# One transpose of the input instead of two: the residual rebuilt from the normalised rows

## The chip, the core and the metric

The kernel runs on one NeuronCore of a Trainium2 chip. The metric is the device time of one launch in microseconds (us), as the median of three runs. The core has five engines that run side by side, each through its own list of instructions in order: PE multiplies matrices and transposes, ACT and DVE read what PE leaves in its accumulator banks (PSUM), POOL works on the on-chip memory (SBUF) alone, and SP issues DMAs. "PEld" in the profile is PE's load of the stationary operand.

## What is computed

One layer of a decoder, for 1024 prompt rows and 32 sample rows (8 sequences of 4 tokens), D = 1024:

```python
def mixer_inputs(x, pos, ln_w, w_in, ...):
    z = rmsnorm(x, ln_w) @ w_in            # rmsnorm: x * rsqrt(mean(x*x) + EPS) * w
    ...                                    # retention q/k/v/gate, MLA latents, gates
def finish_layer(x, ret_o, rg, mla_o, mg, ga, gb, ple, ...):
    h_ret = retention_out(ret_o, rg, ret_gn_w) @ w_down_ret
    h_mla = (mla_o * jax.nn.silu(mg)) @ w_down_mla
    merged = jax.nn.sigmoid(ga) * h_ret + jax.nn.sigmoid(gb) * h_mla
    x = x + merged @ w_out                 # the residual: raw x
    return x + jax.nn.sigmoid(x @ w_ple_gate) * (ple @ w_ple_proj)
```

So the raw rows x are needed twice: normalised at the start, and unchanged as the residual of the output projection near the end.

## The kernel before, in words

All 1056 rows (NT) are kept transposed: features on the 128 partitions, rows along the free axis. Every product is computed in three passes with operands split into a high and a low part (`mac`, L262 to L268: high by high, high by low, low by high).

**The head (L332 to L469).** The rows come in nine tiles of 128 (the ninth, tile 8, has the 32 sample rows). `norm_tile(t)` (L332) squares and sums a tile on ACT (L337), gets the reciprocal root r of each row through `rstd_of` (L233, L235, on POOL but for the first tile), and then makes two transposed copies:

- the raw one: `turn_input` (L314) transposes the eight 128x128 blocks of the tile on PE (L322) in two halves of four, each half into one PSUM bank of the kind `tr` (there are three), ACT copies each bank to SBUF (L323), and SP stores it to the scratch tensor xTD in DRAM (L324);
- the normalised one: DVE multiplies the rows by r (L340, tile xs), PE transposes the eight blocks (L345), again in two banks, and for each block ACT writes the high part times the weight of the norm (L350, xh) and DVE the low part (L351, xl). These stay in SBUF as the operand xn of all input projections.

`latent_tile(t)` (L373) then multiplies the tile by the latent weights, 24 matmuls of 384 columns and 24 of 320 into two banks `ac` (also three). ACT, POOL and DVE normalise and rotate the result (L385, L233, L235, L387, L361 to L366), PE transposes it five times (L396, L398, two banks `tr`), ACT and DVE copy it out (L400, L401). `turn_p(t)` (L326) transposes the tile of a second input with two more transposes through the same `turn_input` (tile names pl and pTD). The tiles go in the order 0, 1, 8, 2, 3, 4, 5, 6, 7, and `norm_tile` runs two tiles ahead of `latent_tile`. From the seventh tile on, the gate projections (`fill`, L421) are woven in.

**The end (L1303 to L1377).** The down projections are merged, and the output projection runs for eight feature blocks f: while block f multiplies, SP loads block f+1 of xTD (`x_transposed`, L1298, from a pool `w4` with three slots), and DVE adds it to each third of the product (L1365). Tiles of the size of one block come from a pool of 23 slots (`xs_`).

**What sets the order.** The program text gives priorities. A list scheduler walks it ahead of the run with estimated times, gives out slots and banks as they come free in that estimate, and writes one fixed list of instructions for each engine; at run time an engine goes through its list in order and waits where an instruction is not ready. So a change of the text can change the order on every engine.

Of the kernel before, what the change touches and what calls it, by code (L numbers as in the profile page):

```python
# [9 lines left out]
F32 = mybir.dt.float32  # L10
# [4 lines left out]
ALU = mybir.AluOpType  # L15
# [4 lines left out]
P = 128  # L20
D = 1024
# [4 lines left out]
NT = SEQ + NR  # L26
# [128 lines left out]
def run(g):  # L155
    for _ in g:
        pass
# [3 lines left out]
def decode_step(ctx: ExitStack, tc: tile.TileContext, A: dict, O: dict):  # L161
    nc = tc.nc
    pe, act, dve, pool, sp = nc.tensor, nc.scalar, nc.vector, nc.gpsimd, nc.sync
# [3 lines left out]
    dram = ctx.enter_context(tc.tile_pool(name="scratch", bufs=1, space=DRAM))  # L167
# [11 lines left out]
    def tr():  # L179
        return banks["pool"].tile([P, 512], F32, tag="tr", name="tr", bufs=3)  # L180
# [6 lines left out]
    def slots(pl, tag, bufs):  # L187

        return lambda name, shape=(P, NT), dt=F32R: pl.tile(list(shape), dt, tag=tag, name=name, bufs=bufs)

    def b32(ap):
        return ap.bitcast(F32)
# [26 lines left out]
    vD = [dram.tile([P, NT], F32, tag=f"v{f}", name=f"v{f}") for f in range(4)]  # L219
    latD = dram.tile([P, 5, SEQ], F32, tag="latD", name="latD")  # L220
    xTD = dram.tile([P, 8, NT], F32, tag="xTD", name="xTD")
    pTD = dram.tile([P, 2, NT], F32, tag="pTD", name="pTD")
    krD = dram.tile([P, 8, ROPE], F32, tag="krD", name="krD")

# [2 lines left out]
    def small(pl, tag, w=1, bufs=4):  # L227
        return pl.tile([P, w], F32, tag=tag, name=tag, bufs=bufs)

    def rstd_of(pl, ss, n, scale, by=pool, w=1):  # L230

        v = small(pl, f"rs_v{w}", w, 4 if w == 1 else 2)
        by.tensor_scalar(v[:n], ss[:n], scale, EPS, op0=ALU.mult, op1=ALU.add)  # L233
        r = small(pl, f"rs_r{w}", w, 4 if w == 1 else 2)
        pool.tensor_tensor(out=r[:n], in0=v[:n], in1=nhalf[:n].to_broadcast([n, w]), op=ALU.pow)  # L235
        return r
# [16 lines left out]
    def load_w(src, nk):  # L253

        hi, lo = wtiles()
        src = src.rearrange("(k p) f -> p k f", p=P)
        for k in range(0, nk, 4):
            ks = slice(k, min(k + 4, nk))
            stage(src[:, ks], hi[:, ks], lo[:, ks])
        return hi, lo  # L260
# [9 lines left out]
    def gemm(w, xs, evac, nk, thirds_=range(3)):  # L270

        for j in thirds_:
            ps = mm()
            sl = slice(j * TH, (j + 1) * TH)
            for k in range(nk):
                mac(ps[:, :TH], (w[0][:, k, :], w[1][:, k, :]), (xs[k][0][:, sl], xs[k][1][:, sl]), k == 0, k == nk - 1)
                if k == nk - 1:
                    evac(j, ps[:, :TH], sl)
                yield 0.441
# [6 lines left out]
    p1 = ph.enter_context(tc.tile_pool(name="p1", bufs=2))  # L286
# [3 lines left out]
    def rows(t):  # L290
        return P if t < 8 else NR
# [22 lines left out]
    def turn_input(t, src, dst, nf):  # L314

        n = rows(t)
        for half in range(0, nf, 4):
            st = p1.tile([P, 4, P], F32, tag="turn", name="turn", bufs=4)
            w = min(4, nf - half)
            pt = tr()  # L320
            for i in range(w):
                pe.transpose(pt[:, i * P:i * P + n], src[:n, (half + i) * P:(half + i + 1) * P], ident[:n, :n])  # L322
            act.copy(st[:, :w, :n], pt[:, :w * P].rearrange("p (a b) -> p a b", a=w)[:, :, :n])  # L323
            sp.dma_start(dst[:, half:half + w, t * P:t * P + n], st[:, :w, :n])  # L324
# [7 lines left out]
    def norm_tile(t):  # L332
        n = rows(t)
        xt = xts.pop(t)
        ss = small(p1, "ss")
        xs = p1.tile([P, D], F32, tag="xs", name="xs", bufs=2)
        act.activation(xs[:n], xt[:n], AF.Square, accum_out=ss[:n])  # L337
        r = rstd_of(p1, ss, n, 1.0 / D, dve if t == 0 else pool)
        turn_input(t, xt, xTD, D // P)
        dve.tensor_scalar(xs[:n], xt[:n], r[:n], None, op0=ALU.mult)  # L340
        for half in range(2):
            pt = tr()
            for q in range(4):
                k = half * 4 + q
                pe.transpose(pt[:, q * P:q * P + n], xs[:n, k * P:(k + 1) * P], ident[:n, :n])  # L345
            for q in range(4):
                k = half * 4 + q
                src = pt[:, q * P:q * P + n]
                hi = xn[k][0][:, t * P:t * P + n]
                act.activation(hi, src, AF.Copy, scale=lnw[:, k:k + 1])  # L350
                dve.scalar_tensor_tensor(out=xn[k][1][:, t * P:t * P + n], in0=src, scalar=lnw[:, k:k + 1],  # L351
                                         in1=b32(hi), op0=ALU.mult, op1=ALU.subtract)

    def rope_nat(out, z, t, n, pl, nh, tag):

        cos = ropeM[:n, t, 0:32].unsqueeze(1).to_broadcast([n, nh, 32])
        sin = ropeM[:n, t, 32:64].unsqueeze(1).to_broadcast([n, nh, 32])
        t1 = pl.tile([P, nh, 32], F32, tag=tag + "1", name=tag + "1", bufs=1)
        t2 = pl.tile([P, nh, 32], F32, tag=tag + "2", name=tag + "2", bufs=1)
        x1, x2 = z[:, :, 0:32], z[:, :, 32:64]  # L360
        dve.tensor_tensor(out=t1[:n], in0=x1, in1=cos, op=ALU.mult)  # L361
        dve.tensor_tensor(out=t2[:n], in0=x2, in1=sin, op=ALU.mult)
        dve.tensor_tensor(out=out[:, :, 0:32], in0=t1[:n], in1=t2[:n], op=ALU.subtract)
        dve.tensor_tensor(out=t1[:n], in0=x2, in1=cos, op=ALU.mult)
        dve.tensor_tensor(out=t2[:n], in0=x1, in1=sin, op=ALU.mult)
        dve.tensor_tensor(out=out[:, :, 32:64], in0=t1[:n], in1=t2[:n], op=ALU.add)  # L366
# [68 lines left out]
    sp.dma_start(cst[:, :head], A["consts"][:, :head])  # L435
    sp.dma_start(lnw, A["ln_w"][0].rearrange("(f p) -> p f", p=P))
    norm_tile(0)
    order = [0, 1, 8, 2, 3, 4, 5, 6, 7]
    for k in range(8):
# [4 lines left out]
    sp.dma_start(kvw, A["kv_norm_w"][0:1, :].to_broadcast([P, KL]))  # L444
    sp.dma_start(ropeM, A["ropeM"])
    norm_tile(order[1])
    load_x(order[3])

    def latents():
        due = iter(())  # L450
        for n, t in enumerate(order):
            tile_ = latent_tile(t)
            next(tile_, None)
            run(due)
            due = tile_
            if n + 2 < 9:
                norm_tile(order[n + 2])
            if n + 4 < 9:
                load_x(order[n + 4])
            turn_p(t)  # L460
            if n == 1:
                sp.dma_start(cst[:, head:], A["consts"][:, head:])
                sp.dma_start(gnw, A["ret_gn_w"][0].rearrange("(f p) -> p f", p=P))
            if n == 4:
                page_rows()
            yield 7.1 if n > 5 else 0.0
        run(due)
# [523 lines left out]
    def split(raw, hi, lo):  # L991
        act.copy(hi, raw)
        lo_of(lo, raw, hi)
        return hi, lo
# [236 lines left out]
    for h in range(HM):  # L1231
# [15 lines left out]
        for n, m in enumerate((3, 2, 0, 1)):  # L1247
            back = waiting.pop(0) if waiting and (h + 1 < HM or n != 1) else iter(())
# [24 lines left out]
    xs_, w4 = slots(pz, "x", 23), slots(pz, "w4", 3)  # L1273
# [14 lines left out]
    def load_gated(f, pl):  # L1288
        lo = gated(f, pl)
        return split_gated(pl("gh"), lo)  # L1290

    def gate(src, f):
        t = w4("gate", dt=F32)
        sp.dma_start(t, src[f])
        act.activation(t, t, AF.Sigmoid)
        return t

    def x_transposed(f):  # L1298
        xT = w4("xT", dt=F32)
        sp.dma_start(xT, xTD[:, f, :])  # L1300
        return xT

    M, gx = [], []  # L1303
    for f in range(8):
# [3 lines left out]
        out = M[f]  # L1308
# [9 lines left out]
    for half in range(2):  # L1318
        for f in range(8):
            w = load_w(A["w_down_ret"][0, half * 1024:(half + 1) * 1024, f * P:(f + 1) * P], 8)  # L1320
            ga = gate(gaD, f)
            if half:
                merged.append((xs_("mh"), xs_("ml")))

            def evac(j, ps, sl, f=f, ga=ga, half=half):
                t = wst.tile([P, TH], F32, tag="gev", name="mev", bufs=2)
                dve.tensor_tensor(out=t, in0=ps, in1=ga[:, sl], op=ALU.mult)
                out = M[f][:, sl]
                dve.tensor_tensor(out=out, in0=out, in1=t, op=ALU.add)
                if half:  # L1330
                    split(out, merged[f][0][:, sl], merged[f][1][:, sl])
            if half and f == 7:
                nxt_xT = x_transposed(0)
            run(gemm(w, gx, evac, 8))
            if half == 0:
                nxt.append(load_gated(8 + f, xr_))
        gx = nxt
# [18 lines left out]
    for f in range(8):  # L1356
        fs = slice(f * P, (f + 1) * P)
        xT = nxt_xT
# [125 lines left out]
```

## Time and profile before

| | us |
|---|---|
| median of 3 runs | 2250.8 |
| lowest, highest run | 2250.61, 2253.29 |
| the profiled execution | 2248.48 |
| its span, first to last instruction | 2246.7 |
| PE busy in the span | 2192.1 |

The trace gives start and length of each instruction in us from the start of the span. A row of the timeline reads: start, length, engine, line, operation, tile written and tiles read, form, count, and in brackets the idle time of the engine before it with what ended it. Matmuls are pipelined: the length of one (0.3 us) is longer than the step from one to the next, so costs on PE are taken from starts.

### The profile page before, as it was taken

What the parts mean: (1) busy time and instruction counts of PE and PEld (TensorE: products, weight loads), DVE (VectorE), ACT (ScalarE), POOL (GpSimd) and SP (SyncE); (2) the same over time, 40 slices, a digit from 0 to 9 for tenths busy, and PEclk for the clock granted to TensorE, in tenths of its full rate; (3) what the DMA queues carried; (4) which work ended last, traced back from release to release, by engine and by line L of the source; (5) the groups of instructions that cost most, each with busy time, mean ns of one, the idle gap of its engine ahead of it and who ended that gap; (6) DMA issues with size and microseconds to landing.
All of it is one profiled execution on the core that took longest, in us unless ns stands there. A gap on an engine that the chain in (4) does not pass through costs nothing.

```text
span 2246.7 us, 45040 instructions
## 1 busy us (share of the span) xinstructions
PE 2192.1 (98%) x18482; PEld 1975.0 (88%) x18482; DVE 1207.9 (54%) x2624; ACT 709.8 (32%) x1532; POOL 509.9 (23%) x682
## 2 busy tenths in 40 slices
PE   8899999999999999999999999999999999999997
PEld 7898888888888899798798779888887999999997
DVE  5414454444544438728638447767767344454465
ACT  6312112222322123222222122355456332222243
POOL 2224434344444114203203102122222000000021
PEclk9999999999999999999999999999999999999999
DMA  8446565656565442532613753200110453333243
GB/s 234 131 148 247 184 223 174 227 183 222 182 232 178 153 135 59 165 99 66 212 49 95 237 162 87 81 23 24 37 46 27 149 192 106 96 94 107 87 141 114
DMA packets 293391, 303.65 MB, mean 135 GB/s; under 512 B 29760, under 2 KB 242048, under 8 KB 293184
## 3 DMA queue, kind: packets, MB, share of 16 engines
q1 hardware_dynamic: 268608, 216.86, 31.3%
q0 software_dynamic: 24576, 83.90, 10.8%
q8 instruction: 145, 2.38, 0.4%
q14 instruction: 62, 0.51, 0.1%
HBM read 234.76 MB, written 65.94 MB: 134 GB/s over the span
## 4 chain that ended last, share of the span: by engine, by line
PE 82%; DVE 7%; issue 6%; POOL 3%; ACT 2%; DMA 1%; SPq 0%; POOLq 0%; ACTq 0%; DVEq 0%
PE mm L266 19%; PE mm L268 18%; PE mm L267 18%; PE sc L640 5%; PE x L667 3%; PE mm L1199 2%; PE ac L267 2%; PE ac L268 2%; PE ac L266 2%; PE tr L1186 1%; PE ac L936 1%; PE ac L932 1%; DVE Stl L198 1%; PE ac L1139 1%; PE tr L791 1%
## 5 line engine op out<-in xcount | busy, mean ns | idle before, releaser
L266 PE MATMUL mm<-xh,wh 128*128 128x352 f32 x1728 | 577.4, 334 | 0.2 <-ACT qq L523 0.2
L268 PE MATMUL mm<-xh,wl 128*128 128x352 f32 x1728 | 562.4, 325 | 0.0
L267 PE MATMUL mm<-xl,wh 128*128 128x352 f32 x1728 | 560.5, 324 | 0.0
L266 PEld LDWEIGHTS mm<-xh,wh 128*128 128x128 f32 x1728 | 324.6, 188 | 38.4 <-issue 29.5
L268 PEld LDWEIGHTS mm<-xh,wl 128*128 128x128 f32 x1728 | 325.5, 188 | 18.6 <-issue 17.3
L267 PEld LDWEIGHTS mm<-xl,wh 128*128 128x128 f32 x1728 | 325.8, 189 | 14.5 <-issue 7.2
L198 DVE TENSOR_TENSOR wl<-wr,wh 128x512 fp32r<-128x512 f32 (+2 forms) x283 | 189.0, 679 | 202.4 <-ACT wh L247 175.7
L247 ACT CAST wh<-wr 128x512 fp32r<-128x512 f32 x248 | 149.8, 619 | 356.0 <-PE mm L267 319.2
L634 DVE STREAM_TRANSPOSE kt<-craw 128x512 f32<-128x512 f32 x256 | 159.3, 679 | 151.0 <-PE sc L640 150.4
L413 ACT ACTIVATE gev<-mm 128x352 f32<-128x352 f32 x132 | 61.1, 463 | 357.2 <-PE mm L268 256.7
L584 POOL DMA_INDIRECT rraw<-in_cache_krope_dram,idx x128 | 123.7, 966 | 215.4 <-DVE kt L634 166.2
L585 POOL DMA_INDIRECT craw<-in_cache_ckv_dram,idx x128 | 120.5, 941 | 142.6 <-PE x L667 102.2
L640 PE MATMUL sc<-kt,q 32*32 32x256 f32 x5120 | 125.5, 385 | 0.1
L266 PE MATMUL mm<-mh,wh 128*128 128x352 f32 x384 | 124.3, 324 | 0.8 <-DVE M L1309 0.8
L267 PE MATMUL mm<-ml,wh 128*128 128x352 f32 x384 | 124.5, 324 | 0.0
L268 PE MATMUL mm<-gh,wl 128*128 128x352 f32 x384 | 124.3, 324 | 0.0
L266 PE MATMUL mm<-gh,wh 128*128 128x352 f32 x384 | 124.3, 324 | 0.0
L268 PE MATMUL mm<-mh,wl 128*128 128x352 f32 x384 | 124.2, 324 | 0.0
L267 PE MATMUL mm<-gl,wh 128*128 128x352 f32 x384 | 124.1, 323 | 0.0
L1415 POOL TENSOR_TENSOR xr<-x1h,x1l 128x352 f32<-128x352 f32 x24 | 26.1, 1106 | 404.7 <-PE mm L268 367.0
L640 PEld LDWEIGHTS sc<-kt,q 32*32 32x32 f32 x5120 | 75.1, 103 | 34.0 <-issue 9.5
L1164 POOL TENSOR_SCALAR pr<-pr,rl 128x896 f32<-128x896 f32 (+3 forms) x64 | 49.7, 777 | 133.3 <-DVE rl L1163 91.0
(351 smaller groups left out, 4294.4 us busy)
## 6 DMA issues: line engine op xcount, KB each, us to landing
wr<-in_w_in_dram SPq DMA_DIRECT2D x144, 256.0 KB, 3.6
st<-in_state_ret_dram SPq DMA_DIRECT2D x32, 512.0 KB, 5.2
out_ret_sample_dram<-st SPq DMA_DIRECT2D x32, 512.0 KB, 3.3
wr<-in_w_ple_gate_dram SPq DMA_DIRECT2D x48, 256.0 KB, 3.0
gt<-gev SPq DMA_DIRECT2D x48, 176.0 KB, 3.3
gl<-go SPq DMA_DIRECT2D x16, 528.0 KB, 4.2
gate<-ga SPq DMA_DIRECT2D x16, 528.0 KB, 3.5
g<-gt SPq DMA_DIRECT2D x32, 256.0 KB, 3.2
```

The lines of the kernel that those rows point to most:

```text
L198: dve.tensor_tensor(out=out, in0=src, in1=b32(hi), op=ALU.subtract)
L247: hi_by[0](hi, raw)
L266: pe.matmul(out, wh, xh, start=first, stop=False)
L267: pe.matmul(out, wh, xl, start=False, stop=False)
L268: pe.matmul(out, wl, xh, start=False, stop=last)
L413: act.activation(t, ps, func)
L584: pool.indirect_dma_start(out=r[:, i], out_offset=None, in_=rows_r, in_offset=off)
L585: pool.indirect_dma_start(out=c[:, i], out_offset=None, in_=rows_c, in_offset=off)
L634: dve.transpose(t.rearrange("p j (n r) -> p n j r", r=32), src.rearrange("p n (j r) -> p n j r", r=32))
L640: pe.matmul(sc[32 * s:32 * s + 32, q, :], Q["q4"][qs_, j + i, s, :], kt[s][qs_, i, :], start=n + i == 0, stop=n == NJ // 2 - 1 and i == 1, ...
L667: pe.matmul(pv[32 * s:32 * s + 32, :KL], pT[:, n, 32 * s:32 * s + 32], keys[s][:, n, :], start=n == 0, stop=n == 4 * NK - 1, tile_position ...
L1164: pool.tensor_scalar(p_[:, :W], p_[:, :W], rl, 1.0, op0=ALU.mult, op1=ALU.mult)
```

## The change

The raw rows are no longer transposed. In `norm_tile` the call of `turn_input` goes; DVE takes the reciprocal of r for each row, and SP stores this column of up to 128 numbers to a new scratch row rmsD. The normalised tile is transposed as before, and when the high and low parts of a half are made, ACT also copies that bank, and SP stores the copy to xTD. So xTD now holds x times r instead of x. At the end rmsD is loaded once, spread over all partitions, and POOL multiplies each loaded block of xTD by it.

```diff
+    rmsD = dram.tile([1, NT], F32, tag="rmsD", name="rmsD")
...
         r = rstd_of(p1, ss, n, 1.0 / D, dve if t == 0 else pool)
-        turn_input(t, xt, xTD, D // P)
+        back = small(p1, "rms")
+        dve.reciprocal(back[:n], r[:n])
+        sp.dma_start(rmsD[0, t * P:t * P + n].unsqueeze(1), back[:n])
         dve.tensor_scalar(xs[:n], xt[:n], r[:n], None, op0=ALU.mult)
...
                 dve.scalar_tensor_tensor(out=xn[k][1][:, t * P:t * P + n], in0=src, scalar=lnw[:, k:k + 1],
                                          in1=b32(hi), op0=ALU.mult, op1=ALU.subtract)
+            st = p1.tile([P, 4, P], F32, tag="turn", name="turn", bufs=4)
+            act.copy(st[:, :, :n], pt.rearrange("p (a b) -> p a b", a=4)[:, :, :n])
+            sp.dma_start(xTD[:, half * 4:half * 4 + 4, t * P:t * P + n], st[:, :, :n])
...
         sp.dma_start(xT, xTD[:, f, :])
+        pool.tensor_tensor(out=xT, in0=xT, in1=rms, op=ALU.mult)
         return xT
...
             if half and f == 7:
+                rms = xs_("rms", dt=F32)
+                sp.dma_start(rms, rmsD.to_broadcast([P, NT]))
                 nxt_xT = x_transposed(0)
```

## The prediction

> **What bounds the kernel now.** I read the page first, for the span and the engines' shares.
>
> ```profile
> span 2246.7 us, 45040 instructions
> PE 2192.1 (98%) x18482; PEld 1975.0 (88%) x18482; DVE 1207.9 (54%) x2624; ACT 709.8 (32%) x1532; POOL 509.9 (23%) x682
> ```
>
> PE is busy 98% of the span. That says that work taken from PE can count, not that it does: it counts where PE stands at the limit, and the change touches only two places. So next comes the table of busy time by stretch. I chose the edges: 24 us is where the latent weights are all there, 96 where the last transposes of x rows are done, 2020 to 2115 the output projection.
>
> ```profile
> core 0: us, PE busy (x) PEld busy (x) DVE busy (x) ACT busy (x) POOL busy (x), PEclk, DMA share, GB/s
> 4.70:24.00 19.30, 17.61 (x97) 14.87 (x98) 12.47 (x26) 13.60 (x34) 5.29 (x8) 1.00 0.93 285
> 24.00:96.00 72.00, 64.44 (x435) 58.54 (x434) 38.94 (x127) 37.71 (x113) 19.43 (x46) 1.00 0.62 176
> 96.00:145.00 49.00, 49.00 (x309) 48.99 (x309) 10.22 (x29) 9.04 (x27) 5.36 (x12) 1.00 0.30 90
> 2020.00:2115.00 95.00, 95.00 (x589) 95.00 (x589) 39.50 (x71) 23.36 (x46) 4.64 (x5) 1.00 0.34 102
> ```
>
> Right behind the head PE has no gap at all (49.00 of 49.00), so time won in the head is kept as long as the lists behind it stay alike. Within the head PE idles 72.00 - 64.44 = 7.6 us of 72. What it waits for there, with the two groups of transposes:
>
> ```profile
> PE tr L345 <- DVE la L363: 3.2, 4, 1.7
> PE tr L345 <- DVE xs L340: 2.3, 2, 1.7
> PE tr L322 <- DVE lt L401: 1.7, 1, 1.7
> PE tr L345 <- DVE latS L363: 0.4, 1, 0.4
> L322 PE MATMUL tr<-cst,xt 128*128 128x128 f32 x48 | 7.1, 277 | 1.8 <-DVE lt L401 1.7
> L345 PE MATMUL tr<-cst,xs 128*128 128x128 f32 x48 | 6.4, 277 | 5.2 <-DVE la L363 2.6 <-DVE xs L340 2.3 <-DVE latS L363 0.4
> ```
>
> All of it is at transposes: 5.9 us until DVE has made the normalised rows xs (the row names la L363 where that instruction stands behind xs on DVE), and 1.7 us until a `tr` bank is free. One tile in order of time, on PE:
>
> ```profile
> 79.89 0.49 PE L396 MATMUL tr<-cst,la 128*128 128x128 f32 x3
> 80.22 0.38 PE L398 MATMUL tr<-cst,la 128*128 128x128 f32 x2
> 80.44 1.27 PE L322 MATMUL tr<-cst,xt 128*128 128x128 f32 x8
> 81.46 0.42 PE L266 MATMUL ac<-wlh,xh 128*128 128x384 f32 x1
> ...
> 82.59 0.34 PE L266 MATMUL ac<-wlh,xh 128*128 128x384 f32 x1
> 83.32 1.06 PE L345 MATMUL tr<-cst,xs 128*128 128x128 f32 x8 [0.39 <-DVE la L363]
> ```
>
> The eight raw transposes come right behind the latent product, then seven matmuls of the next tile, then PE reaches the normalised transposes and waits 0.39 us. That is the question of the case: if the raw ones go, do matmuls move up into their place, or does PE wait longer for xs?
>
> **The change part by part.**
>
> *Removed: 72 transposes on PE.* In the stretch 24 to 96 there are 48 of them, six groups of eight. The group above takes 81.46 - 80.44 = 1.02 us of PE's list. The cheapest end is the first group:
>
> ```profile
> 33.13 1.04 PE L322 MATMUL tr<-cst,xt 128*128 128x128 f32 x8
> 33.93 0.42 PE L266 MATMUL ac<-wlh,xh 128*32 128x384 f32 x1
> ```
>
> 0.80 us. Six groups are 4.8 to 6.1 us; I take 0.9 each, **5.4 us**. I count it whole because the list is drawn anew: the scheduler puts the normalised transposes where it thinks that xs is ready, and fills what is before with matmuls of the next tile, as it already does with seven of them here. The lateness of xs against that estimate then stays what it is.
>
> The other 24 are in the first 24 us.
>
> ```profile
> 4.71 1.94 PE L322 MATMUL tr<-cst,xt 128*128 128x128 f32 x8 [4.71 <-DMA cst<-in_consts_dram]
> 7.22 1.97 PE L345 MATMUL tr<-cst,xs 128*128 128x128 f32 x8 [0.56 <-DVE xs L340]
> 8.98 0.67 PE L322 MATMUL tr<-cst,xt 128*128 128x128 f32 x4
> 10.22 0.44 PE L266 MATMUL ac<-wlh,xh 128*128 128x384 f32 x1 [0.57 <-ACT xh L350]
> 20.89 0.78 POOL L195 TENSOR_SCALAR wlh<-wlr 128x704 fp32r<-128x704 f32 x1 [4.16 <-DMA wlr<-in_w_in_dram]
> PEld ac L267 <- DVE wll L198: 0.4, 2, 0.2
> ```
>
> The first eight lie before a wait for xs and the next four before a wait for ACT, so they cost nothing. The last twelve, four full and eight of the 32-row tile, would be 1.2 us at a tenth each, but the last slice of the latent weights lands only at 20.89, and PE waits for slices even now. I take 0, with both ends 0 and 1.2.
>
> *Removed: two of seven banks for each tile.* Raw transposes no longer take `tr` banks, so the one wait of 1.73 us at L322 for a bank has no instruction left. Whether PE then stands at xs instead is open, as that tile's L345 waited 1.7 us too. Ends 0 and 1.7; I take **0.9**.
>
> *Added: nine reciprocals on DVE.*
>
> ```profile
> L1163 DVE RECIPROCAL rl<-l x64: 147/163/167, 1463.7 to 1732.8; 128x1 f32<-128x1 f32 x64
> ```
>
> 0.16 us each. Only the first stands on the path, ahead of the first xs, for which PE waits at 7.22: **+0.2**. For the others DVE is free 33 us of 72; without that cover all nine would be 1.5 us.
>
> *Moved: the 18 copies on ACT.* They are as many and of the same form as before, but now they read the bank of the normalised blocks, behind its last low part.
>
> ```profile
> 85.75 0.63 ACT L350 ACTIVATE xh<-tr,lnw 128x128 fp32r<-128x128 f32 x2 [0.16 <-DVE xl L351]
> 86.53 0.63 ACT L350 ACTIVATE xh<-tr,lnw 128x128 fp32r<-128x128 f32 x2 [0.16 <-DVE xl L351]
> 86.15 0.61 DVE L351 SCALAR_TENSOR_TENSOR xl<-tr,lnw,xh 128x128 fp32r<-128x128 f32 x2 [0.18 <-ACT xh L350]
> 86.93 0.61 DVE L351 SCALAR_TENSOR_TENSOR xl<-tr,lnw,xh 128x128 fp32r<-128x128 f32 x2 [0.18 <-ACT xh L350]
> 90.94 0.49 PE L396 MATMUL tr<-cst,la 128*128 128x128 f32 x3
> L323 ACT COPY turn<-tr 128x512 f32<-128x512 f32 (+2 forms) x19 | 9.2, 501 | 1.1 <-PE tr L322 0.4
> ```
>
> ACT and DVE take turns, two blocks at a time, one from each of the two banks: a high part never runs beside the low part of its own bank. So a copy starts only when the fourth low part is done, and the bank is held for one copy more, about 0.6 us (9.2 us for 19, the wide ones more). Nothing behind waits for the copy's data; what can wait is PE, for the bank. I take 0, because the tile shown makes its last low parts from 86.93 to 87.54 and the next banks are asked for at 90.94; the other end is a rival below.
>
> The Trainium skill, "PSUM — Partial Sum Buffer", section "PSUM bank collisions raise a hardware error", says that no two of PE, ACT and DVE may touch one bank in the same quadrant at once, reads included. The alternation above agrees with it. By that rule no shorter hold is to be had from any order: the copy adds its whole length to each bank.
>
> *Added: nine stores of a column on SP, and the two xTD stores of a tile issued later.* The nearest row is the store of 128 pieces of 256 bytes:
>
> ```profile
> L392 SPq DMA_DIRECT2D krD<-la x8: 423/436/448, 28.4 to 141.2; - x8
> ```
>
> 0.44 us of SP for each, 4 us in all, which nobody on PE counts. But SP is a list as well: the new store waits for the reciprocal, and behind it stand loads of x rows and weights. Since r of a tile is made two tiles ahead, I take 0; the other end is 0.44 us for each of nine x tiles, 4.0.
>
> *Added at the end: one spread load, eight products on POOL.*
>
> ```profile
> L1300 SPq DMA_DIRECT2D xT<-xTD x8: 338/338/339, 1994.5 to 2076.0; - x8
> L1365 DVE TENSOR_TENSOR x<-mm,xT x24: 523/524/525, 2021.2 to 2110.4; 128x352 f32<-128x352 f32 x24
> L747 POOL TENSOR_TENSOR k<-k,rt x12: 1152/1162/3153, 841.7 to 1251.4; 128x352 f32<-128x352 f32 x12
> ```
>
> The product is three times as wide as L747's, so at most 3 x 1.16 = 3.5 us, between a load issued at 1994.5 and its use at 2021.2, 26.7 us later. Even with two transfers and three times that price it is covered; POOL has 4.64 of 95 us busy there. I take 0; without the cover it would be 8 x 3.5 = 28 us.
>
> *Sum.* -5.4 - 0.9 + 0.2 = **-6.1 us**. On the profiled execution that is 2248.5 - 6.1 = 2242.4 us. The median of the runs is 2.3 us above that execution, and I forecast the median: 2250.8 - 6.1 = **2244.7 us**.
>
> **The rivals.**
>
> *A. The wait for xs takes what the transposes leave.* If the matmuls don't move up, PE reaches L345 a group earlier and waits a group longer, since xs is set by the chain ACT, POOL, DVE. For it: seven waits at L345 with 5.9 us stand in the row already. Against it: the seven matmuls ahead of L345 show that the list is filled by estimate. Then only a part of the bank wait is won, 2250.8 - 0.9 + 0.2 = 2250.1 us.
>
> *B. The banks are held too long: slower.* A tile needs five banks of three, and two of them are now freed only after the copy. Where ACT's or DVE's list has other work between the low parts, the hold grows: the tile whose transposes start at 72.65 makes its last low part at 79.46, and PE asks for banks at 79.89.
>
> ```profile
> 79.46 0.35 DVE L351 SCALAR_TENSOR_TENSOR xl<-tr,lnw,xh 128x128 fp32r<-128x128 f32 x1 [0.44 <-ACT xh L350]
> ```
>
> There the margin is 0.1 us and the copy takes 0.6. If every one of the eight full tiles pays a bank wait as long as the one in the list of waits, 8 x 1.73 = 13.8, the sum is +7.7: 2258.5 us. It decides against the change from 0.8 us a tile (6.1 over 8). The skill's rule on banks stands behind this one. Against it: two bank requests of a tile are gone, and the tile at 84 has 3 us of margin.
>
> *C. The waits go with the work.* A redrawn list could also place L345 late enough that its 5.9 us vanish, with the whole 1.7: 5.4 + 5.9 + 1.7 - 0.2 = 12.8, 2238.0 us. Nothing but the new order speaks for it.
>
> **How the numbers follow.** Forecast 0.52 (2242 with every term at its good end, 6.1 + 1.7 + 1.2 - 0.2 = 8.8, to 2248), A 0.26, B 0.14, C 0.08. What a measurement can tell from no change is about 0.2%, 4.5 us. Faster than 2246.3: most of the forecast (0.47), C 0.08 and 0.02 of A, 0.57. Slower than 2255.3: 0.12 of B. The rest, 0.31, within. The range runs from 2239, which takes in the forecast's good end and the edge of C, to 2254, which is A with the 4.0 of SP's stores; outside are the rest of C and most of B, under 0.2.
>
> **What would show it.** Right: no L322 rows with xt; in the stretch of the head's six middle tiles PE's instructions fall by 48, and the end of the head comes 5 to 7 us earlier; more than seven matmuls between the latent transposes and L345; the waits at L345 still near 6 us. A shows as waits at L345 near 11 us. B shows as PE waits at L396, L398 or L345 released by ACT's new copy. The POOL products should end 15 us or more before L1365 needs them. Wrong altogether would be a change of gaps between 145 and 2115 us, where no step of mine lies.

## The result, and the profile after

The change made the kernel slower: 2272.7 us as the median of four runs, beside 2251.5 for the kernel before (one run more than in the table above). The ratio is 1.0092, with a 95% interval of 1.0078 to 1.0105. I had forecast 2244.7, with a range of 2239 to 2254.

The page of the changed kernel shows that the work on PE did get less, and the time more:

```profile
span 2269.7 us, 44928 instructions
PE 2193.0 (97%) x18410; PEld 1976.9 (87%) x18410; DVE 1223.1 (54%) x2633; ACT 709.5 (31%) x1532; POOL 527.5 (23%) x690
```

The 72 raw transposes are gone (18482 instructions on PE before, 18410 now). Busy time hardly moved: in part of the head the granted clock was lower (0.91 from 24 to 96 us), and what PE ran there took longer. The table by stretch, with the edges of before (the output projection now lies 23 us later), says where the time went. The columns are those of the tables above: stretch and its length, busy time and instructions of PE, PEld, DVE, ACT and POOL, the granted clock, the DMA engines' busy share, and GB/s:

```profile
4.70:24.00 19.30, 8.50 (x30) 7.70 (x31) 8.75 (x19) 8.37 (x19) 4.74 (x7) 1.00 0.91 199
24.00:96.00 72.00, 55.57 (x318) 50.18 (x318) 32.62 (x107) 31.40 (x94) 14.63 (x35) 0.91 0.84 156
96.00:145.00 49.00, 47.12 (x305) 46.20 (x304) 17.21 (x55) 17.61 (x53) 7.49 (x19) 1.00 0.60 119
2043.00:2138.00 95.00, 95.00 (x593) 95.00 (x592) 49.56 (x71) 23.39 (x46) 19.52 (x11) 1.00 0.34 104
```

Most of it is in the head. In the first 24 us PE ran 30 instructions instead of 97, from 24 to 96 it ran 318 instead of 435. The output projection is as full as before (95.00 of 95.00). The last store of the latents (latD) marks the end of the head, first in the kernel before, then in the changed one:

```profile
L402 SPq DMA_DIRECT2D latD<-lt x8: 525/525/526, 34.6 to 152.4; - x8
L408 SPq DMA_DIRECT2D latD<-lt x8: 518/519/581, 46.0 to 170.6; - x8
```

It comes 18.2 us later, of the 23.0 us by which the span is longer; where the other 4.8 us arise behind it is left open.

One pair of columns in the table goes apart: in the stretch 24 to 96 the DMA engines are busier than before (0.84 beside 0.62) and move less (156 GB/s beside 176). Ten microseconds of the start, first of the changed kernel:

```profile
10.00:20.00 10.00, 6.34 (x23) 5.53 (x23) 5.41 (x10) 3.01 (x8) 3.15 (x4) 1.00 0.92 85
```

then of the kernel before:

```profile
10.00:20.00 10.00, 9.24 (x53) 7.64 (x54) 8.80 (x19) 7.90 (x22) 3.57 (x5) 1.00 0.84 238
```

92% busy for 85 GB/s beside 84% for 238. Just ahead of this stretch SP issued the first of the new column stores, at 9.99 us. The rows of that line (start of the first and last, and the time from issue to landing):

```profile
L342 SPq DMA_DIRECT2D rmsD<-rms x9: 318/437/638, 10.0 to 115.4; - x9
...
DMA to landing us min/median/max: 8.3/8.9/9.2
```

Half a kilobyte takes 8.3 to 9.2 us to land, in the five of nine cases for which the trace has a landing. The store that I had taken as the nearest row, 32 KB in pieces of 256 bytes, took this long in the kernel before (two of its eight have a landing):

```profile
DMA to landing us min/median/max: 1.5/1.5/1.6
```

Loads that were issued behind a column store were late as well. For the three slices of the latent weights (wlr) that SP issued between 10 and 16 us, the changed kernel has

```profile
DMA to landing us min/median/max: 7.2/9.8/10.3
```

and for slices issued at the same time a version without column stores (the one with one row store, below; two of its three have a landing) has

```profile
DMA to landing us min/median/max: 2.9/3.0/3.2
```

The waits of PE in the first 115 us of the changed kernel (waiting line, what it waited for, us in total, times, longest):

```profile
PE tr L348 <- DVE xs L343: 12.5, 3, 10.7
PE tr L402 <- ACT turn L357: 6.8, 2, 6.2
PE tr L323 <- DMA pl<-in_p_sample_dram: 3.6, 1, 3.6
PE ac L267 <- ACT xh L353: 3.6, 1, 3.6
PE tr L323 <- DMA pl<-in_p_prompt_dram: 3.2, 1, 3.2
...
PE tr L404 <- ACT turn L357: 0.5, 1, 0.5
```

Three suspects stand in this list. **S**: the column stores clog the DMA engines, and loads are late (waits for pl, and for xh and xs through the weights). **C**: the moved copies hold the `tr` banks (L402 and L404 wait for the copy, L357, 7.3 us). **D**: the new order on DVE puts the first weight split ahead of the first normalised rows, so that PE comes to the first normalised transposes at 10.7 us instead of 7.2.

### The profile page after: what moved, and what is told of

Same layout as the page of the kernel before. It is cut to its first block, busy times and chain, and to the rows that moved or that the text cites. A ratio compares the mean times of both kernels' runs of the same rounds, so it can differ in the third digit from the quotient of the medians.

```text
span 2269.7 us, 44928 instructions
## 1 busy us (share of the span) xinstructions
PE 2193.0 (97%) x18410; PEld 1976.9 (87%) x18410; DVE 1223.1 (54%) x2633; ACT 709.5 (31%) x1532; POOL 527.5 (23%) x690
## 3 DMA queue, kind: packets, MB, share of 16 engines
q0 software_dynamic: 24576, 83.90, 10.6%
## 4 chain that ended last, share of the span: by engine, by line
PE 80%; DVE 7%; issue 5%; DMA 3%; POOL 2%; ACT 2%; SPq 0%; POOLq 0%; ACTq 0%; DVEq 0%
PE mm L267 19%; PE mm L269 18%; PE mm L268 18%; PE sc L646 5%; PE x L673 3%; PE mm L1205 2%; PE ac L268 2%; PE ac L269 1%; PE ac L267 1%; PE tr L1192 1%; PE ac L942 1%; PE ac L938 1%; DVE Stl L198 1%; PE ac L1145 1%; PE tr L797 1%
## 5 line engine op out<-in xcount | busy, mean ns | idle before, releaser
L1307 POOL TENSOR_TENSOR xT<-xT,rms 128x1056 f32<-128x1056 f32 x8 | 20.0, 2504 | 323.0 <-DMA rms<-rmsD 263.1
```

## The experiments

The first set ran on a chip on which the kernel before takes 2252.8 us. The second and third ran on chips on which it takes 2429.3 and 2430.2 us at a mean granted clock of 0.96, so their times are read only beside the kernel before of the same set.

**The column stores alone.** The kernel before, with all its raw transposes, plus the reciprocals and the stores, which nobody reads:

```diff
...
         turn_input(t, xt, xTD, D // P)
+        back = small(p1, "rms")
+        dve.reciprocal(back[:n], r[:n])
+        sp.dma_start(rmsD[0, t * P:t * P + n].unsqueeze(1), back[:n])
```

> The kernel before, raw transposes and all, plus the nine reciprocals and the nine column stores of 128 pieces of 4 bytes, which nobody reads. Theory S (the column stores block the DMA queues: each lands after 8.3 to 9.2 us in the changed kernel, 9 x 8.9 = 80 us in a head of 96): 12 to 24 us slower than before, about 2263 to 2275, and the latent weights' loads land later than 5.4 us. Theory C (the copies, now on the normalised banks, hold PSUM too long: PE waits 7.3 us for them in the changed kernel): within 3 us of before. Theory D (DVE's list now has the first weight split ahead of the first normalised tile, so PE starts at 10.67 instead of 7.22 us): within 3 us of before, since this kernel keeps the old place of the copies.

Measured: 2280.2 us, ratio 1.0129 (1.0111 to 1.0148), 27.5 us slower. Its table by stretch has the same mark as the changed kernel, with nothing added but the reciprocals and the stores:

```profile
4.70:24.00 19.30, 13.70 (x59) 12.01 (x60) 8.99 (x19) 10.40 (x23) 4.34 (x6) 0.82 0.94 208
24.00:96.00 72.00, 53.95 (x317) 47.23 (x316) 32.50 (x104) 29.03 (x86) 15.43 (x35) 0.88 0.81 152
```

S holds, with a loss 3.5 us above the upper end that I had set; C and D alone would have left this kernel where it was. The trace has no landing of a slice of the latent weights, but POOL waited up to 8.30 us for one, where its longest such wait before was 4.16.

**One row store.** The changed kernel, but the reciprocals are gathered in one tile, transposed once by PE behind the head, and stored as nine pieces of 512 bytes:

```diff
...
-        back = small(p1, "rms")
-        dve.reciprocal(back[:n], r[:n])
-        sp.dma_start(rmsD[0, t * P:t * P + n].unsqueeze(1), back[:n])
+        dve.reciprocal(backs[:n, t:t + 1], r[:n])
...
     beside(latents(), 3 * 7.1, fill, 36)
+    pb = tr()
+    pe.transpose(pb[:9, :P], backs, ident)
+    rows9 = p1.tile([9, P], F32, tag="rows9", name="rows9", bufs=1)
+    act.copy(rows9, pb[:9, :P])
+    sp.dma_start(rmsD[0].rearrange("(t p) -> t p", p=P), rows9)
```

> The changed kernel, but the reciprocals are gathered as columns of one tile, transposed once by PE behind the head and stored as nine pieces of 512 bytes; no column store. Theory S: the loss goes and what I forecast for the change comes out, 2 to 8 us faster than before, 2243 to 2249. Theory C: still 10 us or more slower than before. Theory D: the loss of the start stays, 3 to 10 us above the forecast of S, 2247 to 2258.

Measured: 2245.0 us, ratio 0.9967 (0.9954 to 0.9980), 7.8 us faster than before. So the stores, with the row store in their place, are 29 us of the changed kernel (21.2 above before, and 7.8 below it without them), and what is left of the change is a gain. This version beats both kernels.

**The order on DVE.** The same, with the weight splits kept behind the first normalised rows in DVE's list:

```diff
...
-        lo_of(lo, raw, hi)
+        with tc.issue_after(getattr(first[0], "ins", first[0])):
+            lo_of(lo, raw, hi)
...
```

> As the one before, and DVE's weight splits are kept behind the first normalised tile in its list. Theory S alone: the same time as the one before, within 2 us. Theory D: 3 to 8 us faster than the one before, and PE starts its first transposes near 7.4 us instead of 10.7. Theory C: still 10 us or more slower than the kernel before the change.

Measured: 2245.6 us, ratio 0.9969 (0.9956 to 0.9982). PE starts its first transposes at 7.4 instead of 10.6 us, and the end does not move. D falls. A likely reason, which no run shows, is that the start waits for the latent weights: POOL begins on the last slice at 21.2 us here and at 20.8 with the row store. The waits of PE with one row store, in the first 120 us, answer C:

```profile
PE tr L348 <- DVE xs L343: 11.7, 2, 10.6
PE tr L348 <- DVE la L369: 4.4, 5, 1.9
PE tr L404 <- ACT turn L357: 2.0, 3, 1.0
PE tr L402 <- ACT turn L357: 0.7, 1, 0.7
```

The copies still hold PE up, for 2.7 us, and that is inside the gain. The first row counts the whole time from the start of the span to the first transposes.

And the longest wait for a copy in the changed kernel, 6.2 us at L402, does not begin at the copy. The rows that lead to it, in order of time:

```profile
84.60 0.62 POOL L195 TENSOR_SCALAR wh<-wr 128x512 fp32r<-128x512 f32 x1 [6.94 <-DMA wr<-in_w_in_dram]
85.25 0.69 DVE L198 TENSOR_TENSOR wl<-wr,wh 128x512 fp32r<-128x512 f32 x1 [4.34 <-POOL wh L195]
...
86.24 1.07 ACT L357 COPY turn<-tr 128x512 f32<-128x512 f32 x2 [4.73 <-DVE xl L354]
86.88 0.90 PE L402 MATMUL tr<-cst,la 128*128 128x128 f32 x3 [6.16 <-ACT turn L357]
```

POOL waited for a slice of weights (wr) that SP had issued at 76.32 us, right behind a column store at 75.89. DVE's split of that slice waited for POOL, the last low parts (xl) stood behind the split in DVE's list, the copy waited for them, and PE for the copy. So most of what I had put down to C is S as well: the name in the wait is only the last link.

**What in the store costs: the first probe.** The kernel before with seven small stores in the quiet output projection, one behind each block f:

```diff
+        if f == 0:
+            sp.dma_start(flat(pA, 1), pr[:, :1])
+        if f == 1:
+            sp.dma_start(pB[:, :1], pr[:, :1])
...
+        if f == 5:
+            sp.dma_start(flat(pF, 1)[:32], pr[:32, :1])
```

> The kernel before, with one probe store behind each of seven blocks of the output projection, where the queues are a third busy, to scratch that nobody reads: 128 pieces of 4 bytes side by side; 128 of 4 bytes each 512 bytes apart; 128 of 64 bytes side by side; 128 of 512; 128 of 4 bytes each 64 bytes apart; 32 of 4 bytes side by side; 128 of 256. If the cost is the number of small pieces in one 512-byte line, written one after another at 8.9 us / 128 = 70 ns, then the first lands after about 9 us, the sixth after about 3.5, the fifth after 3 or less, the second as fast as the 256-byte one (1.5 to 2 us). If it is the smallness of a piece alone, the first, second and fifth all take about 9 us. If it is only the crowd of other transfers in the head, all land within 3 us.

Inconclusive for the store that mattered: the trace gives no landing for three of the seven, the first among them, since nothing waited for them. It had 2.0 us for 512 bytes apart and 5.3 for 32 pieces side by side. So each store was given a load that reads it back:

> The kernel before with seven probe stores in the output projection, each now followed by a load of the same place, so that its landing is awaited: 128 pieces of 4 bytes side by side; 128 of 4 bytes 512 bytes apart; 128 of 4 bytes 64 bytes apart; 32 of 4 bytes side by side; 128 of 64 side by side; 128 of 256; 128 of 512. The first probe gave 2.0 us for 512 bytes apart, 5.3 for 32 side by side, 2.9 for 64 bytes side by side. Theory of the shared line (small pieces that fall into one line of DRAM are written one after another): 8 to 10 us for the first, 2 for the second, 2 to 3.5 for the third (eight pieces to a line), 5.3 again for the fourth. Theory of small pieces as such: the first three alike, 8 to 10.

SP's waits for the seven landings, by the line of the load. In the order of the expectation the lines are 1377, 1380, 1383, 1386, 1389, 1392, 1395:

```profile
SPq L1377 <- DMA pA<-x1h: 7.9, 1, 7.9
...
SPq L1386 <- DMA pF<-x1h: 3.5, 1, 3.5
SPq L1380 <- DMA pB<-x1h: 2.1, 1, 2.1
SPq L1389 <- DMA pC<-x1h: 2.0, 1, 2.0
SPq L1392 <- DMA pG<-x1h: 1.9, 1, 1.9
SPq L1383 <- DMA pE<-x1h: 1.7, 1, 1.7
SPq L1395 <- DMA pD<-x1h: 1.6, 1, 1.6
```

Of these seven only 4-byte pieces side by side are slow, in a quiet stretch too. As many pieces of 4 bytes, 64 or 512 bytes apart, are as quick as pieces of 512 bytes. Smallness as such falls. Each probe ran once, and 32 pieces took 5.3 us from issue to landing in the first probe but 3.5 us of waiting here; that difference is not explained.

**The stores apart, in the head.** The stores alone once more, each piece 512 bytes from the next:

```diff
-    rmsD = dram.tile([1, NT], F32, tag="rmsD", name="rmsD")
+    rmsD = dram.tile([NT, 128], F32, tag="rmsD", name="rmsD")
...
-        sp.dma_start(rmsD[0, t * P:t * P + n].unsqueeze(1), back[:n])
+        sp.dma_start(rmsD[t * P:t * P + n, :1], back[:n])
```

> The kernel before plus reciprocals and nine column stores that nobody reads, as in the run that was 1.3% slower, but each 4-byte piece goes to a place 512 bytes from the next. As many pieces, the same instructions. Theory of the shared line: the loss goes, within 4 us of before, and each store lands in 2 to 3 us. Theory of small pieces as such: again 20 to 35 us slower.

Measured: ratio 1.0014 (1.0004 to 1.0024), 4.1 us above before by the medians, where side by side cost 1.3%. Instructions, pieces and bytes are the same; nine tenths of the loss went with the spacing. SP still has nine stores that wait for their reciprocals, so all that these cost apart from the neighbouring pieces is in the 4.1 us (1.0 to 5.8 by the interval). Its trace has no landing times, as nothing waits for these stores.

**The late column.** The row store's kernel, but the gathered reciprocals leave as one column store of 1152 pieces behind the head:

```diff
-    pb = tr()
-    pe.transpose(pb[:9, :P], backs, ident)
-    rows9 = p1.tile([9, P], F32, tag="rows9", name="rows9", bufs=1)
-    act.copy(rows9, pb[:9, :P])
-    sp.dma_start(rmsD[0].rearrange("(t p) -> t p", p=P), rows9)
+    sp.dma_start(rmsD[0].rearrange("(t p) -> p t", p=P), backs)
```

> The faster kernel, but the gathered reciprocals leave as one column store of 1152 pieces of 4 bytes behind the head, among the weight loads of the gate projections. If the small pieces are written one after another wherever they stand, it lands after about 1152 x 70 ns = 80 us, holds the weight loads back meanwhile, and the kernel is 20 to 75 us slower than with the row store. If the place in the tight head was what cost, within 4 us of the row store, 2241 to 2249.

Measured: ratio 0.9956 (0.9939 to 0.9972), as fast as the row store on the two other chips (0.9967 and 0.9966). Of my two theories the first, with 80 us to land and a loss of 20 to 75 us, was wrong, and the second came true as far as ratios from different chips can be compared. Its stretches around the store, issued at 93.4 us:

```profile
97.00:101.00 4.00, 4.00 (x27) 4.00 (x26) 0.96 (x3) 2.49 (x8) 0.00 (x0) 1.00 0.59 26
101.00:105.00 4.00, 4.00 (x27) 4.00 (x26) 0.00 (x0) 0.24 (x1) 0.49 (x1) 1.00 1.09 92
105.00:109.00 4.00, 4.00 (x26) 4.00 (x25) 1.69 (x2) 0.46 (x1) 0.71 (x2) 1.00 0.88 219
```

The mark of the clog is there (0.59 busy for 26 GB/s, then 1.09 for 92), but it lasts about 10 us, no longer than that of a store with a ninth of the pieces, so it isn't 70 ns a piece. (Neighbours in DRAM come from neighbouring partitions, as in the nine stores; the nine pieces of one partition lie 512 bytes apart. The share adds up the time of packets and can pass 1.) And PE is full throughout, 4.00 of 4.00: no load that it needed then came late. So in these runs the clog cost time in the head, where PE lives on loads that are just arriving, and none here.

**The first three stores.** The stores alone, for tiles 0, 1 and 8 only:

```diff
-        sp.dma_start(rmsD[0, t * P:t * P + n].unsqueeze(1), back[:n])
+        if t in (0, 1, 8):
+            sp.dma_start(rmsD[0, t * P:t * P + n].unsqueeze(1), back[:n])
```

> The kernel before plus the column stores of the first three tiles alone (0, 1 and the 32-row tile); the other six tiles make none. All nine cost 28 us. If the start is where it hurts, because the latent weights come in there: 12 to 20 us slower. If every store costs alike: 28 x 3 / 9 = 9 us slower, 7 to 11. If the later six do it: under 4 us.

Measured: ratio 1.0043 (1.0024 to 1.0061), 10.8 us by the medians, 3.6 a store; all nine cost 27.5, 3.1 a store. That speaks for a loss spread over the head rather than one due to the start, though the interval, 5.8 to 14.8 us, reaches into the 12 to 20 that I had given to the start.

**The transposes put back.** The row store's kernel with the 72 raw transposes on PE again, unread and not copied:

```diff
+        for half in range(2):
+            pt = tr()
+            for i in range(4):
+                pe.transpose(pt[:, i * P:i * P + n], xt[:n, (half * 4 + i) * P:(half * 4 + i + 1) * P], ident[:n, :n])
         dve.reciprocal(backs[:n, t:t + 1], r[:n])
```

In the second set it ran beside the late column:

> The faster kernel with one row store, and the 72 raw transposes put back on PE; their result is read by nobody and is not copied. My sum has 5.4 us for the transposes and 0.9 for the banks: 4 to 8 us slower than without them, 2249 to 2253. If the waits at the normalised transposes take up what the raw ones leave (rival A), less than 2 us.

and in the third beside the row store itself:

> The changed kernel with one row store, once more, beside the next one on the same chip (the second set of runs was on a chip on which the kernel before takes 2429 us instead of 2251, so its times stand only beside each other). 0.2 to 0.45% faster than before.

> The same with the 72 raw transposes put back, unread. On the slower chip it was 3.4 us above the kernel with a late column, whose own difference to the row store is not known. My sum: 4 to 8 us slower than the row store. Rival A: less than 2 us.

Measured, second set: ratio 0.9977 (0.9967 to 0.9987), 3.4 us above the late column. Third set: the row store 0.9966 (0.9954 to 0.9979), the transposes back 0.9985 (0.9971 to 1.0000), 4.4 us between the medians. The intervals overlap a little and the two profiled executions of the third set are alike, so it is a likely 3 to 4 us, not a sharp figure. Both differences are above the 2 us of rival A, but not clear of it, and 3.4 lies under the 4 to 8 that I expected.

**A ladder of spacings.** Probes with read-back again, at more steps and counts:

```diff
+            sp.dma_start(flat(q8, 2)[:128, :1], pr[:128, :1])
+            sp.dma_start(spare[:128, :1], flat(q8, 2)[:128, :1])
...
+            sp.dma_start(flat(q4n64, 1)[:64, :1], pr[:64, :1])
+            sp.dma_start(spare[:64, :1], flat(q4n64, 1)[:64, :1])
```

> Probes with read-back as before: 128 pieces of 4 bytes at steps of 4, 8, 16 and 32 bytes, then 16 and 64 pieces at a step of 4, then 32 pieces at 64. So far: step 4 with 128 pieces 7.9 us of waiting, with 32 pieces 3.5, steps of 64 and 512 1.7 and 2.1. If the pieces that share a 64-byte block are written one after another, at (7.9 - 1.7) / 16 = 0.4 us each: 7.9, 4.8, 3.3, 2.5 for the four steps, 8 for 64 pieces and for 16 alike, 1.7 for the last. If what counts is the number of pieces at a step under 64 bytes, whatever the step: 7.9 for all four, 2.6 for 16 pieces, 4.8 for 64, 1.7 for the last.

SP's waits; 1377 to 1386 are 128 pieces at steps of 4, 8, 16 and 32 bytes, 1389 and 1392 are 16 and 64 pieces at a step of 4, 1395 is 32 pieces at 64:

```profile
SPq L1377 <- DMA q<-x1h: 7.8, 1, 7.8
SPq L1392 <- DMA q4n<-x1h: 6.0, 1, 6.0
SPq L1380 <- DMA q<-x1h: 4.3, 1, 4.3
SPq L1386 <- DMA q<-x1h: 1.9, 1, 1.9
SPq L1389 <- DMA q4n<-x1h: 1.7, 1, 1.7
SPq L1383 <- DMA q<-x1h: 1.5, 1, 1.5
SPq L1395 <- DMA q64n<-x1h: 1.5, 1, 1.5
```

Neither rule fits. Steps of 16 and 32 are free, so the number of pieces alone does not decide; 16 pieces side by side are free as well, where the rule of 64-byte blocks wanted 8 us, and 32 (in the set of probes before this one), 64 and 128 take 3.5, 6.0 and 7.8. Each of these, too, ran once. What the pieces collide in stays open.

## Why the prediction was wrong

**The step that failed: the column stores.** I wrote "0.44 us of SP for each, 4 us in all, which nobody on PE counts", took 0, and set the other end at 4.0 us. Measured, they cost 27.5 us alone and 29 in the changed kernel. I priced the issue on SP and took the landing for granted, by a row with pieces of 256 bytes. What I had priced, issues and waits on SP, is within the 4.1 us of the stores apart; the rest is the clog, behind which a weight slice landed after 7.2 to 10.3 us instead of 2.9 to 3.2. No row of before stores pieces of 4 bytes, so this was an operation that the trace did not show; its bound from above should have been open, and the fact that the DMA engines were 0.93 busy in the first 24 us, a row that I had quoted, should have told me what a blocked engine is worth there. The loss lies outside the range and outside every rival: B has a loss too, but by another mechanism. The Trainium skill, "DMA: Bandwidth & Descriptors", section "Specifications", says that below 512 bytes the DMA does a read-modify-write. The probes agree only in part: 128 pieces of 256 and of 64 bytes were awaited for 1.9 and 2.0 us, as short as pieces of 512; by that rule alone my row would have been the right one.

**The transposes.** I took 5.4 us for them, whole, because matmuls would move up into their place. In the row store they do: behind the latent transposes stand thirteen matmuls, where the tile that I showed had seven, and then the normalised transposes.

```profile
79.05 0.38 PE L404 MATMUL tr<-cst,la 128*128 128x128 f32 x2
...
82.32 1.06 PE L348 MATMUL tr<-cst,xs 128*128 128x128 f32 x8 [0.61 <-DVE la L369]
```

But PE waits longer as well. Between 24 and 96 us it idles 7.8 us without the raw transposes and 5.7 with them put back (third set; 8.1 and 5.8 in the second, with the late column); in the third set its waits at the normalised transposes alone are 5.0 and 3.2. So about 2 us of the 5.4 went to waits, which is rival A in part, and the 3.3 that are left are near the 3.4 and 4.4 between the medians. By the last store of latD the head ends only 0.9 us (second set) and 1.9 us (third) earlier without them. The step was half right: the matmuls moved up, but "the lateness of xs against that estimate then stays what it is" did not hold, and the term was too large.

**The sum without the stores** was -6.1 us, and the kernel with one row store is 7.8 faster, with an interval of 4.5 to 10.4 (0.46% and 0.20% of 2252.8). So the total of the rest came out, but in part by luck. The sum has its whole gain in the head, and I had asked for an end of the head 5 to 7 us earlier; the last store of latD is issued at 149.6 us, 2.8 earlier than before. The rest of the 5.5 us between the two profiled executions (spans of 2246.7 and 2241.2) arises behind the head, where no term of mine lies. The parts moved too: the head of the row store, by stretch,

```profile
4.70:24.00 19.30, 12.27 (x62) 11.65 (x63) 12.33 (x25) 10.63 (x24) 5.39 (x7) 1.00 0.79 252
24.00:96.00 72.00, 64.15 (x416) 57.83 (x415) 41.34 (x141) 40.55 (x125) 18.84 (x46) 1.00 0.66 182
```

has PE idle for 7.0 us of the first 19.3, where it was 1.7, and hardly more idle than before after that (7.9 beside 7.6).

**The start.** I added 0.2 us for a reciprocal ahead of the first rows. I missed that in the new order DVE's list has a weight split ahead of these rows, so that PE comes to the normalised transposes 3.4 us later (10.67 instead of 7.22); why the scheduler drew it so was not looked into. Undoing it did not move the end.

**Rival A** (the wait takes it all) did not come true as I put it: with the row store the waits at the normalised transposes behind the first are 5.0 us (4.4 and 0.6) between 24 and 96, not 11; what it took is the 2 us above. **Rival B** had a real place: PE waits 2.7 us for the copies in the row store. The price of 13.8 was five times too high, and in the changed kernel, where these waits are 7.3, taking the stores away brought them down with nothing done to the copies: 6.2 of the 7.3 go back to the late slice shown above.

**The end** went as told: the products take 2.47 us each (I had at most 3.5), and the output projection has no gap. The line of the product and, of its tile, the use on DVE:

```profile
L1307 POOL TENSOR_TENSOR xT<-xT,rms x8: 2463/2473/2706, 2025.5 to 2103.0; 128x1056 f32<-128x1056 f32 x8
L1374 DVE TENSOR_TENSOR x<-mm,xT x24: 509/525/525, 2044.6 to 2133.3; 128x352 f32<-128x352 f32 x24
```

The first product ends 16 us ahead of its first use.

**What stays open.** The clog is shown by the stores alone, the spacing and the late column; how the DMA engines or the memory behind them come to be blocked by neighbouring pieces is not, and neither is what moved behind the head.

## What to carry to other kernels

Here a store cost by the layout of its pieces in DRAM, not by its bytes or its issue. So a column of 4-byte numbers that would lie side by side is better turned on the chip and stored as a row. A DMA share that rises while GB/s falls was the mark of such a store, and it hurt where PE lived on loads that were just arriving. When a trace has no row for the form of a transfer, leave its upper bound open, and probe it before it goes into the tightest stretch.

## What the runs showed of the hardware

128 pieces of 4 bytes at steps of 4 and 8 bytes were awaited for 7.8 and 4.3 us; at steps of 16 bytes and more for 1.5 to 2.1. At a step of 4, 16, 32, 64 and 128 pieces took 1.7, 3.5, 6.0 and 7.8. A store of 1152 such pieces clogged the engines for about 10 us, not longer than one of 128.

A starved PE was also a slower PE. In the changed kernel, matmuls of 384 columns started 0.32 us apart at the start:

```profile
15.79 0.52 PE L267 MATMUL ac<-wlh,xh 128*128 128x384 f32 x1
16.11 0.52 PE L268 MATMUL ac<-wll,xh 128*128 128x384 f32 x1
...
28.80 0.34 PE L268 MATMUL ac<-wll,xh 128*128 128x384 f32 x1
28.97 0.33 PE L269 MATMUL ac<-wlh,xl 128*128 128x384 f32 x1
```

and 0.17 us apart 13 us later. The granted clock between 24 and 96 us was 0.91, where the kernel before had 1.00, and it was low behind stretches in which PE stood still:

```profile
80.00:84.00 4.00, 0.72 (x5) 0.46 (x4) 0.73 (x3) 1.51 (x6) 0.00 (x0) 1.00 0.47 68
84.00:88.00 4.00, 1.12 (x6) 1.13 (x7) 2.53 (x7) 1.35 (x3) 2.13 (x4) 0.59 0.61 137
```

The Trainium skill, "TensorE: Matmul & The Clock Gate", section "What's actually happening", says that PE runs at half clock until it has been busy for a window of about 3.4 us, and falls back after an idle one. The factor of two and these rows agree, and in the trace's clock records of the head the spells at half clock last 3.4 or 6.8 us. At the start the column of the granted clock does not show it: it reads 1.00 from 4.7 to 24 us, where the steps were 0.32 us; the first of these records stands at 26.7 us, just where the steps become short. So part of the 27.5 us is the loads being late, and part the clock that the waits cost (0.82 and 0.88 in the two stretches of the stores alone); the runs do not separate the two.
